# Modulation group 5 is computed in layer 1 in place of block 2

## The chip, the cores and the metric

The kernel runs on one core of a Trainium2 chip. The metric is the device time of one execution in microseconds (us). Five engines work from queues of their own, each strictly in order: TensorE (PE, with PEld for its weight loads), VectorE (DVE), ScalarE (ACT), GpSimd (POOL) and SyncE (SP), which issues nearly all DMA transfers. They wait for each other through semaphores only.

## The reference, cut to what matters

A batch of one sequence with 256 tokens and width 1024 goes through two transformer blocks with a conditioning vector `c` (an NSA attention and a MoBA attention), and then through a third block with windowed and neighbourhood attention and a product-key expert layer (PEER). All is float32. Each norm before a mixer is modulated: a shift and a scale that come from `silu(c) @ w_ada + b_ada` and depend on nothing else.

```python
ada = c_act @ w_ada[layer] + b_ada[layer]
shift1, scale1, gate1, shift2, scale2, gate2 = jnp.split(ada, 6, axis=-1)
h = modulate(rms_norm_2(x, norm1_g[layer]), shift1, scale1)
...
x = x + gate1[:, None, :] * (mixed @ w_out[layer])
h2 = modulate(rms_norm_2(x, norm2_g[layer]), shift2, scale2)
x = x + gate2[:, None, :] * peer(h2, w_query[layer], sub_keys[layer],
                                  u_experts[layer], v_experts[layer])
```

The kernel's modulation group 5 is `shift2, scale2` of this last block: used once, by the norm ahead of `peer`. Group 4 is its gates, used where block 2's output is added to x.

## The kernel before, in words

Four stages follow one another: `layer0` (NSA), `layer1` (MoBA, about 275 to 400 us of the profile), `block2` (to about 540 us) and `peer` (to the end). Tokens are two tiles of 128 rows. Every large product is float32 made of two parts, high and low: a weight tile of 512 KB is loaded (`raw`), ACT casts its high half (`hi`, line 186), DVE subtracts for the low one (`lo`, line 211), and PE runs three matmuls for each product (`mm3`, lines 239 to 241).

Within a stage a list in the table `ORDER` names the steps, and `steps` (line 280) calls them one after the other. A tile scheduler then places the instructions: a step that stands earlier in the list has the earlier priority, and `@n` shifts one by 50 times n. What comes out is one fixed order for each engine. The names in the list that matter here: `z0` to `z3` are the four parts of layer 1's gate projection z, `s...` are attention scores with their softmax, `v..` probabilities times values, `b` the position biases, `o` and `O` the two halves of the output projection. In block 2, `sb0`/`sb1` are the scores and softmax of the neighbourhood attention for the two token tiles (`heads8`, line 1118: scores L1125, row minimum on DVE L1126, exponentials on ACT L1133, normalisation L1139 and L1141), `ob0`/`ob1` their transposes (L1208), copies (L1210) and products with the values (L1214).

`a5` and `a4` are calls of `ada(g)` (line 382), which makes one modulation group: 16 weight tiles of 512 KB, in three buffers (tag `adaw`), each loaded by the SP queue and used by four matmuls into one PSUM tile (`psa`, one buffer); then one DVE addition of the bias, and, for groups 2, 3 and 5, `ada_cols`: four small matmuls (L418), a copy (L422) and a scale (L424).

```python
raw = self.cp.tile([128, 1024], F32, name="adaw", tag="adaw", bufs=CFG["adaw"])
nc.sync.dma_start(raw, a["adaw"][g, k, :, h * 1024:(h + 1) * 1024])            # L391
...
i = nc.tensor.matmul(ps[32 * q:32 * q + 32, ...], self.cond[:, ci + k, :], ...) # L396, 4 for a tile
...
nc.vector.tensor_tensor(r, ps, r, op=OP.add)                                   # L408
```

In the profile one such weight tile is `L396 ... x8` (each of its four float32 matmuls is two records). Both groups 4 and 5 have no input from the token stream, so they can be placed anywhere between the buffers' release and their use.

Of the kernel before, what the change touches and what calls it, by code (L numbers as in the profile page):

```python
# [71 lines left out]
 'cpt0': 2}  # L72
ORDER = {'0': 'pA rt@-4 pB@-4 q0 pC@-2 pG s000 cc z1 ck s001 c00@4 s011 c01 v00 s010 z0 a1@-4 q1 s101@-1 v01@-4 s100 '
      'a2@-4 z2 c10 z3 s110 v10 s111@-2 c11@2 v11 o O a3@-1',
 '1': 'pA@1 q0 s000 s001 v00 q1@-2 s011 s010 v01@-4 z1 s100 z3 s110 s101 z0 z2 b s111 v10@-1 v11@-6 o O',
 '2': 'pA@-2 qa@1 sa0 oa0 kb@-1 qb sa1 oa1 vb tb sb0@5 a4 ob0@1 sb1 a5 o ob1 O@5'}

# [1603 lines left out]
```

## Time and profile before

| | |
|---|---|
| time, median of 3 runs | 1391.27 us (1390.19 to 1397.97) |
| profiled execution, its own time | 1390.83 us |
| its span, first to last instruction | 1389.1 us |
| mean granted PE clock | 0.99 of full speed |
| PE busy | 1339.5 us, 96% of the span |
| DVE busy | 1023.2 us, 74% |
| ACT busy | 820.2 us, 59% |

The share of PE says that the kernel as a whole hangs on PE. It is an average, though: the two places that the change touches have to be read for themselves. In layer 1 at 326 to 354 us PE has hardly a gap. In block 2 it has none before 500 us, some until 517, and a long one at 535 to 540 us, between the last output product and the norm ahead of `peer`.

### The profile page before, as it was taken

The page shows a single profiled execution, that of the slowest core. Times are in us where ns is not written, and L with a number is a line of the kernel's source. Part 1 is how long each engine was busy: PE and PEld are TensorE (multiplying, and loading weights), DVE is VectorE, ACT ScalarE, POOL GpSimd, SP SyncE. Part 2 cuts the span into 40 slices and gives each one's busy share as a digit, 9 for nine tenths or more (in the row PEclk, how much of TensorE's full clock was granted, in tenths as well). Part 3 has the DMA queues.
Part 4 walks back from the last instruction along what each step waited for, and adds up shares of the span by engine and source line. Part 5 has one row for each costly group of instructions (what it writes and reads, how often), then busy time and mean ns, then how long its engine had stood idle before and what let it go on. Part 6 is the DMA issues. An engine that isn't in the chain of part 4 may idle for free.

```text
span 1389.1 us, 25082 instructions
## 1 busy us (share of the span) xinstructions
PE 1339.5 (96%) x8842; PEld 1126.9 (81%) x8842; DVE 1023.2 (74%) x2636; ACT 820.2 (59%) x1887; POOL 21.8 (2%) x27
## 2 busy tenths in 40 slices
PE   6998999999989997999999999999999999999997
PEld 2576775587667756999999999999998888888885
DVE  3595865688576657899999868888866666677777
ACT  3354666367457664555555668888865555555554
POOL 0000000000001100000000000000000000000001
PEclk9999999999999998999999999999999999999999
DMA  8688654742586774555555575455466656667773
GB/s 302 213 283 306 218 188 149 246 157 94 207 296 204 227 236 154 173 179 179 173 180 182 168 217 177 158 166 171 158 224 209 190 192 196 197 222 242 245 242 118
DMA packets 94876, 279.17 MB, mean 201 GB/s; under 512 B 11112, under 2 KB 30320, under 8 KB 94624
## 3 DMA queue, kind: packets, MB, share of 16 engines
q1 hardware_dynamic: 94752, 277.59, 60.6%
q8 instruction: 69, 1.13, 0.3%
q14 instruction: 55, 0.45, 0.1%
HBM read 267.80 MB, written 13.94 MB: 203 GB/s over the span
## 4 chain that ended last, share of the span: by engine, by line
PE 77%; DVE 3%; DMA 2%; ACT 1%; issue 0%; ACTq 0%; DVEq 0%
PE ps L241 18%; PE ps L240 18%; PE ps L239 18%; PE ps L1501 4%; PE acc L241 3%; PE acc L240 3%; PE acc L239 3%; DMA raw<-in_w1o 1%; PE psa L396 1%; PE ps L714 1%; PE ps L525 1%; DVE lo L211 1%; PE ps L709 1%; PE ps L1125 1%; PE ps L639 1%; PE ps L1398 1%
## 5 line engine op out<-in xcount | busy, mean ns | idle before, releaser
L186 ACT CAST hi<-raw 128x512 fp32r<-128x512 f32 (+1 forms) x700 | 429.4, 618 | 350.8 <-PE ps L240 147.8
L211 DVE TENSOR_TENSOR lo<-raw,hi 128x512 fp32r<-128x512 f32 (+1 forms) x700 | 479.8, 688 | 171.2 <-ACT hi L186 158.4
L239 PE MATMUL ps<-hh,hi 128*128 128x256 f32 x1160 | 333.6, 288 | 1.2 <-DVE hh L187 1.2
L240 PE MATMUL ps<-hl,hi 128*128 128x256 f32 x1160 | 329.0, 284 | 1.1 <-DVE hl L211 1.1
L241 PE MATMUL ps<-hh,lo 128*128 128x256 f32 x1160 | 329.0, 284 | 0.0
L239 PEld LDWEIGHTS ps<-hh,hi 128*128 128x128 f32 x1160 | 223.2, 192 | 1.4 <-DVE hh L187 1.4
L240 PEld LDWEIGHTS ps<-hl,hi 128*128 128x128 f32 x1160 | 223.1, 192 | 1.3 <-DVE hl L211 1.3
L241 PEld LDWEIGHTS ps<-hh,lo 128*128 128x128 f32 x1160 | 222.9, 192 | 0.0
L239 PE MATMUL ps<-hi,Ah 128*128 128x512 f32 x508 | 198.1, 390 | 0.0
L240 PE MATMUL ps<-lo,Ah 128*128 128x512 f32 x508 | 197.7, 389 | 0.0
L241 PE MATMUL ps<-hi,Al 128*128 128x512 f32 x508 | 197.6, 389 | 0.0
L240 PEld LDWEIGHTS ps<-lo,Ah 128*128 128x128 f32 x508 | 95.4, 188 | 20.2 <-DVE lo L211 0.2
L239 PEld LDWEIGHTS ps<-hi,Ah 128*128 128x128 f32 x508 | 95.4, 188 | 19.9 <-issue 0.2
L241 PEld LDWEIGHTS ps<-hi,Al 128*128 128x128 f32 x508 | 95.3, 188 | 19.8
L1500 ACT ACTIVATE og<-o,gT 128x128 f32<-128x128 bf16 x256 | 87.2, 394 | 4.1 <-DVE o L1498 0.3
L239 PE MATMUL acc<-hi,hh 128*128 128x512 f32 (+1 forms) x176 | 69.8, 402 | 4.3 <-DVE hh L187 3.1
L240 PE MATMUL acc<-lo,hh 128*128 128x512 f32 (+1 forms) x176 | 70.6, 402 | 2.4 <-DVE lo L211 2.4
L241 PE MATMUL acc<-hi,hl 128*128 128x512 f32 (+1 forms) x176 | 70.2, 400 | 0.0
L1501 PE MATMUL ps<-og,o 128*128 128x128 f32 x512 | 65.1, 275 | 0.0
L1501 PEld LDWEIGHTS ps<-og,o 128*128 128x128 f32 x512 | 61.4, 192 | 0.0
L396 PE MATMUL psa<-adaw,cond 128*32 128x256 f32 x640 | 48.5, 390 | 4.7 <-DMA adaw<-in_adaw 4.3
L1498 DVE TENSOR_TENSOR o<-iof,eT 128x512 bf16<-128x512 f32 x64 | 44.2, 691 | 8.2 <-ACT og L1500 7.5
(397 smaller groups left out, 1937.3 us busy)
## 6 DMA issues: line engine op xcount, KB each, us to landing
raw<-in_u SPq DMA_DIRECT2D x128, 512.0 KB, 3.5
raw<-in_v SPq DMA_DIRECT2D x128, 512.0 KB, 3.5
adaw<-in_adaw SPq DMA_DIRECT2D x86, 512.0 KB, 4.8
raw<-in_w SPq DMA_DIRECT2D x48, 512.0 KB, 3.6
raw<-in_wq SPq DMA_DIRECT2D x16, 512.0 KB, 3.5
zd<-ge SPq DMA_DIRECT2D x56, 128.0 KB, 1.7
ge<-zd SPq DMA_DIRECT2D x56, 128.0 KB, 3.4
raw<-in_adaw SPq DMA_DIRECT2D x10, 512.0 KB, 3.2
```

What stands on the lines that cost most here:

```text
L186: return self.nc.scalar.copy(out, in_)
L211: return self.nc.vector.tensor_tensor(lo, src, hi.bitcast(F32), op=OP.subtract)
L239: mm(out, a[0][asl], b[0][bsl], start=first, stop=False, **kw)
L240: mm(out, a[0][asl], b[1][bsl], start=False, stop=False, **kw)
L241: mm(out, a[1][asl], b[0][bsl], start=False, stop=last, **kw)
L396: i = nc.tensor.matmul(ps[32 * q:32 * q + 32, h * 256:h * 256 + 256], self.cond[:, ci + k, :], raw[:, q * 256:q * 256 + 256], start=(k == ...
L525: self.nc.tensor.matmul(ps[:, k * 128:k * 128 + 128], self.x[t][:, k4 * 512 + k * 128:k4 * 512 + k * 128 + 128], dg, start=(k == 0), stop= ...
L639: nc.tensor.transpose(pr[:P, i * 128:i * 128 + 128], s.rearrange("p a d -> p (a d)") if P == 128 else s, self.identr)
L709: nc.tensor.transpose(ps[:, r * 128:r * 128 + 128], P[a][r][:, br, kb, :], self.c("ident"))
L1498: v.tensor_tensor(o1, iob, eT[0][:, t0:t0 + 4, None].to_broadcast([128, 4, 128]), op=OP.is_equal)
L1500: nc.scalar.activation(og[:, j], o1[:, j], AF.Copy, scale=gT[:, t0 + j:t0 + j + 1])
L1501: nc.tensor.matmul(ps[:, j * 128:j * 128 + 128], o2[:, j], og[:, j], start=(j == 0), stop=(j == 3), skip_group_check=True)
```

## The change

The step `a5` leaves the list of block 2, where it stood behind `sb1`, and enters the list of layer 1, between `z1` and `s100`. The steps themselves are untouched.

```diff
- '1': 'pA@1 q0 s000 s001 v00 q1@-2 s011 s010 v01@-4 z1 s100 z3 s110 s101 z0 z2 b s111 v10@-1 v11@-6 o O',
- '2': 'pA@-2 qa@1 sa0 oa0 kb@-1 qb sa1 oa1 vb tb sb0@5 a4 ob0@1 sb1 a5 o ob1 O@5'}
+ '1': 'pA@1 q0 s000 s001 v00 q1@-2 s011 s010 v01@-4 z1 a5 s100 z3 s110 s101 z0 z2 b s111 v10@-1 v11@-6 o O',
+ '2': 'pA@-2 qa@1 sa0 oa0 kb@-1 qb sa1 oa1 vb tb sb0@5 a4 ob0@1 sb1 o ob1 O@5'}
```

What it does to the order of the engines shows on PE in layer 1. These are the rows before, where scores (`ps<-kT,qT`) and products of z (`acc`) alternate:

```order
1200 L733 MATMUL ps_3558<-kT1_2948,qT_3251 128x256
1201 L240 MATMUL acc_3646<-hl_2868,hi_3699 128x256
1202 L241 MATMUL acc_3646<-hh_2867,lo_3700 128x256
1203 L239 MATMUL acc_3749<-hh_2867,hi_3752 128x256
1204 L240 MATMUL acc_3749<-hl_2868,hi_3752 128x256
1205 L241 MATMUL acc_3749<-hh_2867,lo_3753 128x256
1206 L239 MATMUL acc_3749<-hh_2867,hi_3752 128x256
1207 L733 MATMUL ps_3563<-kT0_2947,qT_3251 128x256
```

And the same place now, with tiles of group 5 (`psa_3717`) between them:

```order
1200 L733 MATMUL ps_3558<-kT1_2948,qT_3251 128x256
1201 L240 MATMUL acc_3646<-hl_2868,hi_3699 128x256
1202 L241 MATMUL acc_3646<-hh_2867,lo_3700 128x256
1203 L396 MATMUL psa_3717<-adaw_3724,cond_82 32x256 x4
1204 L733 MATMUL ps_3563<-kT0_2947,qT_3251 128x256
1205 L733 MATMUL ps_3563<-kT1_2948,qT_3251 128x256
1206 L396 MATMUL psa_3717<-adaw_3730,cond_82 32x256 x4
1207 L733 MATMUL ps_3568<-kT0_2947,qT_3251 128x256
1208 L733 MATMUL ps_3568<-kT1_2948,qT_3251 128x256
1209 L733 MATMUL ps_3585<-kT0_2947,qT_3251 128x256
1210 L733 MATMUL ps_3585<-kT1_2948,qT_3251 128x256
1211 L396 MATMUL psa_3717<-adaw_3736,cond_82 32x256 x4
```

In layer 1, 15 tiles of group 5 (the second to the sixteenth) now stand at rows 1203 to 1318, and L418 follows at row 1324; before there was one tile of group 4 in this place. In turn the 16 tiles of group 4 stand later by two: they take the places that tiles 3 to 16 of group 4 and tiles 1 and 2 of group 5 had. The places of tiles 3 to 16 of group 5, in block 2, are free.

In block 2, before, PE's rows around the first transposes of `ob0` read so (`psa_5525` is group 5, `acc<-hi,ozh0` the first half of the output projection):

```order
1944 L1208 MATMUL ps_5419<-ident_85,P8_5264 128x128 x2
1945 L396 MATMUL psa_5525<-adaw_5586,cond_82 32x256 x4
1946 L1208 MATMUL ps_5419<-ident_85,P8_5264 128x128 x2
1947 L239 MATMUL acc_5706<-hi_5731,ozh0_4461 128x512
1948 L240 MATMUL acc_5706<-lo_5732,ozh0_4461 128x512
1949 L241 MATMUL acc_5706<-hi_5731,ozl0_4462 128x512
1950 L396 MATMUL psa_5525<-adaw_5592,cond_82 32x256 x4
1951 L1214 MATMUL ps_5418<-pt_5424,vb0_4459 64x128 x4
1952 L1208 MATMUL ps_5430<-ident_85,P8_5264 128x128 x4
1953 L1208 MATMUL ps_5441<-ident_85,P8_5264 128x128 x4
1954 L396 MATMUL psa_5525<-adaw_5598,cond_82 32x256 x4
```

Now they read so:

```order
1943 L241 MATMUL acc_5706<-hi_5741,ozl0_4573 128x512
1944 L1125 MATMUL ps_5377<-kT0_4565,qTb0_5339 128x256
1945 L1125 MATMUL ps_5377<-kT1_4566,qTb0_5339 128x256
...
1959 L1125 MATMUL ps_5405<-kT1_4566,qTb0_5339 128x256
1960 L1208 MATMUL ps_5530<-ident_85,P8_5375 128x128 x4
1961 L1214 MATMUL ps_5529<-pt_5535,vb0_4570 64x128 x4
1962 L1208 MATMUL ps_5541<-ident_85,P8_5375 128x128 x4
1963 L1208 MATMUL ps_5552<-ident_85,P8_5375 128x128 x4
1964 L1214 MATMUL ps_5529<-pt_5546,vb0_4570 64x128 x4
```

All 48 products of `o` now come first and without a break (rows 1896 to 1943), then the 16 scores of `sb0`, then `ob0`, then `sb1`, with nothing between them; before, tiles and products were spread among all of these.

On SP, 12 loads of `adaw` now stand between the seventh and the eighth load of z's weights (w1z), and two more behind the eighth, one of them ahead of the output weights w1o. These are the rows:

```order
168 L229 DMA raw_4073<-in_w1z 128x1024 [waits DMAHW5_49,DVE_49]
169 L391 DMA adaw_3742<-in_adaw 128x1024 [waits PE_49]
...
180 L391 DMA adaw_3808<-in_adaw 128x1024 [waits DMAHW2_49,PE_49]
181 L229 DMA raw_4107<-in_w1z 128x1024 [waits DVE_49,Activation_49]
182 L1080 DMA raw_4149<-in_t5c 32x1024 [waits DVE_49]
183 L391 DMA adaw_5427<-in_adaw 128x1024 [waits DMAHW3_49,PE_49]
```

In block 2 the 14 loads of `adaw` that stood between the fourth and the fifth load of the output weights (w2o) are gone from SP.

## Rows read from the trace of the kernel before

**Rows 1.** Page, part 1: busy time, share of the span and instructions by engine.

```profile
PE 1339.5 (96%) x8842; PEld 1126.9 (81%) x8842; DVE 1023.2 (74%) x2636; ACT 820.2 (59%) x1887; POOL 21.8 (2%) x27
```

**Rows 2.** Windows: us; PE, PEld, DVE, ACT, POOL busy; PEclk, DMA share, GB/s.

```profile
326.00:354.40 28.40, 28.32 (x216) 24.62 (x216) 23.39 (x84) 22.93 (x67) 0.00 (x0) 1.00 0.32 114
481.00:512.00 31.00, 30.68 (x261) 18.27 (x259) 12.41 (x44) 14.20 (x36) 0.00 (x0) 1.00 0.86 284
512.00:540.00 28.00, 21.42 (x122) 15.34 (x121) 25.88 (x70) 18.64 (x47) 0.00 (x0) 0.97 0.50 175
```

**Rows 3.** PE timeline, layer 1: start, us, line, operation, tiles, shape, count.

```profile
332.12 0.28 PE L239 MATMUL acc<-hh,hi 128*128 128x256 f32 x1
332.24 0.28 PE L240 MATMUL acc<-hl,hi 128*128 128x256 f32 x1
...
333.24 0.28 PE L239 MATMUL acc<-hh,hi 128*128 128x256 f32 x1
```

**Rows 4.** PE timeline, block 2, 480 to 541 us; in brackets the idle time before.

```profile
480.58 0.47 PE L239 MATMUL acc<-hi,ozh 128*128 128x512 f32 x1
...
482.55 0.40 PE L239 MATMUL acc<-hi,ozh 128*128 128x512 f32 x1
...
483.25 0.39 PE L239 MATMUL acc<-hi,ozh 128*128 128x512 f32 x1
...
488.57 0.39 PE L1125 MATMUL ps<-kT,qTb 128*128 128x256 f32 x1
...
499.05 0.38 PE L1208 MATMUL ps<-ident,P 128*128 128x128 f32 x2
499.36 0.64 PE L396 MATMUL psa<-adaw,cond 128*32 128x256 f32 x8
499.93 0.44 PE L1208 MATMUL ps<-ident,P 128*128 128x128 f32 x2
...
508.21 0.28 PE L1318 MATMUL ps<-cst,osq 128*128 128x1 f32 x2
...
511.28 0.95 PE L418 MATMUL psa<-cst,adar 128*128 128x4 f32 x8
...
517.33 1.24 PE L1208 MATMUL ps<-ident,P 128*128 128x128 f32 x4 [1.22 <-DVE P L1141]
...
540.27 0.98 PE L525 MATMUL ps<-diag,x 128*128 128x128 f32 x3 [4.94 <-DVE rx L274]
```

**Rows 5.** Layer 1's scores on PE, 325.1 to 354.35 us, by line and shape.

```profile
L733 PE MATMUL ps<-kT,qT 128*128 128x256 f32 x24 | 5.0, 295 | 0.0
...
L733 PE MATMUL ps<-kT,qT 128*128 128x128 f32 x16 | 2.8, 285 | 0.1
```

**Rows 6.** The tile `adaw`, 470 to 512 us: from issue to landing.

```profile
DMA to landing us min/median/max: 3.1/4.5/4.7
```

**Rows 7.** ACT timeline, the exponentials of `sb0` and `sb1`.

```profile
489.91 0.51 ACT L1133 ACTIVATE P<-P,nm 128x256 f32<-128x256 f32 x1 [1.43 <-DVE nm L1126]
...
492.35 0.49 ACT L1133 ACTIVATE P<-P,nm 128x256 f32<-128x256 f32 x1
...
492.85 0.49 ACT L1133 ACTIVATE P<-P,nm 128x256 f32<-128x256 f32 x1
...
497.65 0.51 ACT L1133 ACTIVATE P<-P,nm 128x256 f32<-128x256 f32 x1 [1.07 <-DVE nm L1126]
...
511.59 0.51 ACT L1133 ACTIVATE P<-P,nm 128x256 f32<-128x256 f32 x1 [1.54 <-DVE nm L1126]
...
515.40 0.49 ACT L1133 ACTIVATE P<-P,nm 128x256 f32<-128x256 f32 x1
```

**Rows 8.** DVE timeline, block 2: the bias addition of group 5.

```profile
510.38 0.69 DVE L408 TENSOR_TENSOR adar<-psa,adar 128x512 f32<-128x512 f32 x1 [0.78 <-PE psa L396]
```

**Rows 9.** Windows of PE: us, busy, PEclk, DMA share, GB/s.

```profile
398.00:400.00 2.00, 1.75 (x14) 0.65 1.08 362
516.00:518.00 2.00, 0.72 (x4) 1.00 0.00 0
```

## The prediction

> **What bounds the kernel now.** I began with the busy times [rows 1]. PE is busy 1339.5 of 1389.1 us, so at most 50 us of the whole span are not PE's, and a change that only moves PE's work can gain only where PE waits and lose only where it does not. The change removes no instruction. So the second view was the windows over the places where work leaves and where it arrives [rows 2]. Where it arrives, 326 to 354.4 us in layer 1, PE is busy 28.32 of 28.40 us, DVE 23.39 and ACT 22.93. The reader is to see that PE is the full engine there, with the others behind it. Where it leaves, 481 to 512 us in block 2, PE is also full, 30.68 of 31.00, with the transfers at 0.86 of the DMA engines and DVE at only 12.41. The next window, 512 to 540 us, is the opposite: PE 21.42 of 28.00 and DVE 25.88. A full PE has two readings: it may be the bound, or it may be filled with work that could stand anywhere while a chain on other engines sets the pace. The two places differ in this, and the timelines of PE, ACT and DVE tell them apart [rows 3, 4, 7, 8].
>
> **Layer 1: what is added.** The 15 tiles that now stand in this stretch replace one, so 14 are added, and one L418. Between two split products a tile costs this: L240 starts at 332.24 and the L239 that follows the tile and one L241 at 333.24 [rows 3]. That is 1.00 us for two steps that without a tile take 0.12 each (332.12 to 332.24), so the tile takes 0.76. Between scores or transposes it costs 499.93 - 499.36 = 0.57 [rows 4]. By the new order 11 of the 14 stand beside a split product and 3 among scores or transposes: 11 x 0.76 + 3 x 0.57 = 10.1 us. L418 is taken at 0.9 (its own time is 0.95 [rows 4]). Sum 11.0 us.
>
> What could hide part of it is a PE that waits for DVE there without showing it as idle. Only the scores can, since DVE frees their PSUM buffers; they hold PE 5.0 + 2.8 = 7.8 us in all [rows 5]. If a quarter of that is pacing, 2 us are hidden; if nothing, none. I take 0.8, the nearer to the window's full PE.
>
> Two new waits are added. The first is for the weight tiles. Three buffers, and a landing of 3.1 to 4.7 us [rows 6]: at 3.1, near which I put it because the DMA share there is 0.32 and not 0.86 [rows 2], three buffers feed a tile every 1.0 to 1.2 us. The stretch gives 28.4 + 11 us less the part ahead of the first tile, some 20 us for 14 tiles, or 1.4 us each on the mean. It suffices on the mean but not where tiles stand two or three rows apart; I take 0.8 us, with bounds 0 and 4. Queued behind these loads on SP are the eighth w1z load and w1o. The last of the 12 loads must wait for tile 13, some 14 us later than now, and by the order PE first needs the eighth w1z behind the sixteenth tile, so I cost this at nothing; if that cover is missing, one landing of 3 to 5 us is exposed. The second is L408 on DVE, which waits for the sixteenth tile and has scores behind it: in block 2 it waited 0.78 and took 0.69 [rows 8]. PE holds enough products that don't need DVE; 0.2 us, bounds 0 and 1.5.
>
> Layer 1 in sum: 11.0 - 0.8 + 0.8 + 0.2 = +11.2 us, bounds +9 and +15. What follows, the biases, the output projection and the norm of block 2, begins where PE gets through this stretch, so nothing gives it back before block 2. The tiles of group 4 take the places of others of the same kind, tile for tile: nothing.
>
> **Block 2: what is removed.** The same 14 tiles and L418, 11 us of PE. If PE were the bound there to the end, all would come back. But the chain in `sb0`, `ob0`, `sb1` and `ob1` goes over four engines, and the tiles and products stood in its gaps.
>
> First, up to `ob0`. The 48 products of `o` now run in one piece: three take 483.25 - 482.55 = 0.70 us [rows 4], so 11.2. They begin as before at 480.58, plus two tiles that now stand ahead of them (1.1), and end at 493.0 on the clock of before. Only then come the scores of `sb0`, which before began at 488.57. From the first score to the first exponential I take 1.1 (488.57 to 489.91, 1.34, with one product between). Then ACT sets the pace: 0.50 us for each of eight (492.35 to 492.85), so the eighth begins 3.5 us after the first, and from its start to `ob0`'s first transpose pass 499.05 - 497.65 = 1.4 [rows 4, 7]. 493.0 + 1.1 + 3.5 + 1.4 = 499.0, where it stood at 499.05. Gain: 0. Six us of PE's work are gone ahead of this point, and the chain starts as much later.
>
> Second, `ob0`, 499.05 to 508.21, 9.2 us [rows 4]. It is a chain of transposes, copy on ACT, product, four times. Five tiles and five products stand in it. Those that lie under a copy cost nothing; behind a copy's end I count two tiles (0.57 each) and part of a product: gain 1.25.
>
> Third, `sb1`. Before, the first and second exponential were parted by L408 and its tile, and the second began at 511.59, the last at 515.40 [rows 7]. Now: start 1.25 earlier, 506.95; first exponential 1.1 later, seven more at 0.50, and a cast of 0.6 of `ob0`'s result among them: the last begins at 512.3. That is 3.1 earlier, of which 1.85 is new. `ob1` and the rest keep their fillers (the products of `O`) and end as much earlier, with the wait of 4.94 before L525 [rows 4] unchanged, for it is a chain on DVE.
>
> Block 2 in sum: -3.1 us, bounds 0 and -11.
>
> **The sum.** +11.2 - 3.1 = +8.1 us on the profiled execution's own 1390.83 (span 1389.1 and 1.7 around it), which lies 0.44 under the median of 1391.27: 1398.9 us.
>
> **The clock.** At 398 to 400 us the granted clock was 0.65; yet at 516 to 518, where PE was busy 0.72 of 2 us, it kept 1.00 [rows 9]. So gaps of the size that `ob0` and `sb1` get left the clock at the upper of its two levels here, and the sum has no term for it. The Trainium skill speaks against this change at this point ("TensorE: Matmul & The Clock Gate", "HAM oscillation — how this bites in real kernels"): a PE that idles between short bursts finds its clock taken back and runs each next burst at half speed, and it advises to keep matmuls dense. The trace agrees at 400 us and does not at 516. By that rule the result would be the third rival below.
>
> **Rivals.**
>
> First, faster: block 2 gives back nearly all and layer 1 hides part. For it speaks PE at 30.68 of 31.00 up to 512 us [rows 2], with DMA at 0.86, so that the tiles may also have waited for their loads. It needs that `sb0`'s chain starts as early as before. Against it: the new order puts all 48 products ahead of the first score. Price: -11.0 in block 2, +5 to +9 in layer 1: -2 to -6, some 1387. It comes out below 0.5% only if layer 1 hides most of its tiles.
>
> Second, no change: PE is the bound at both ends, +11.2 and -11.0: 1391. For it speaks that PE has no idle record at either place; against it the same order, and that after 512 us it has [rows 2, 4].
>
> Third, slower still: the transposes, products and scores between `ob0` and `ob1`, without fillers, run at half clock. From 499.05 to 517.33 are 18.3 us [rows 4], 15.2 when 3.1 are gone; if a third of that is PE's work at 1.2 GHz instead of 2.4, it takes 5 us more: +13, 1404. It decides from the point at which the gaps let the clock fall. The same time results if the three `adaw` buffers pace layer 1 (the bound of +4 there).
>
> A rival that the change does not do what it says I give no weight: the order shows the tiles moved.
>
> **How the numbers follow.** The forecast has 0.58, the first rival 0.18, the second 0.11, the third 0.13. About 0.5% or 7 us is what a measurement of this kernel tells from no change: 1384.3 and 1398.2. The forecast's own range is 1395 to 1402.5, from its middle bounds (layer 1 +9 to +13, block 2 -2 to -5); 0.6 of it lies above 1398.2. Slower: 0.58 x 0.6 + 0.13 = 0.48. Faster: half of the first rival, 0.09. Same: the rest, 0.43. The range that holds 8 in 10 goes from 1389, which leaves out most of the first rival, to 1404.
>
> **What would show it.** In the profile after, L1084, the first instruction behind the stretch that ends at 354.4 [rows 2], starts 10 to 12 us later, with no idle time of PE for `adaw` over 1 us; L396 there steps by 0.57 to 0.76. The first L1208 of `ob0`, measured from the first product of `o`, stays within 1 us of 499.05 - 480.58 = 18.5; L1318 follows it after 8 us and not 9.2; L525 lies 7 to 9 us later than 540.27. PE shows idle time of some 7 us in block 2 between 493 and 515 that it did not have. I am wrong if L1084 moves by less than 8 us (layer 1 hid work), if `ob0` starts more than 2 us earlier (PE was the bound in block 2), or if the granted clock falls between 495 and 515.

## The result, and the profile after

The changed kernel takes 1409.42 us (median of 11 runs, 1400.26 to 1413.70), the kernel before 1391.04 us beside it (11 runs, 1388.68 to 1397.97). The ratio is 1.0114, 95% interval 1.0096 to 1.0133, so 13 to 19 us slower. The forecast of slower was right, its size was not: 1398.9 was forecast with a range up to 1404.

The page of the changed kernel, part 1, answers to [rows 1]. Its profiled execution took 1410.29 us.

```profile
span 1408.1 us, 25086 instructions
...
PE 1351.8 (96%) x8842; PEld 1137.3 (81%) x8842; DVE 1024.1 (73%) x2636; ACT 822.2 (58%) x1887; POOL 21.9 (2%) x27
```

PE has as many instructions as before, but is busy for 12 us more. The share is again 96%: read alone, it hides both that there is more waiting and that the same matmuls take longer. In layer 1 the first comes from the transfers and the second from the clock. Here is the stretch from the first of the scores (L733) of [rows 5] to L1084 as one window, before and then after (us; PE, PEld, DVE, ACT, POOL busy; PEclk, the granted share of TensorE's full clock; DMA share, GB/s):

```profile
325.10:354.40 29.30, 29.22 (x222) 25.39 (x222) 24.09 (x85) 23.38 (x68) 0.00 (x0) 1.00 0.33 113
```

```profile
327.70:372.70 45.00, 42.06 (x341) 30.74 (x340) 25.32 (x88) 24.94 (x68) 0.00 (x0) 0.92 0.73 237
```

15.7 us longer, where 11.2 were forecast. Idle time of PE is 2.9 us in place of 0.1, the clock is 0.92, and the DMA engines, at a third before, are at 0.73. This is the longest of five executions with the same order in this stretch: the runs e2, e3, e5 and e17 below took 42.1, 44.4, 42.7 and 44.1 us, while without group 5 in it the stretch took 29.3 in each of nine executions. The view of the tile `adaw` in the changed kernel says what PE waits for and how long a load takes (it answers to [rows 6], where the landing was 3.1 to 4.7):

```profile
who waited for it (us, times):
  PEld psa L396: 4.4, 5
  PE psa L396: 2.6, 2
...
DMA to landing us min/median/max: 3.7/5.7/5.9
```

The PE timeline after shows where: the tiles of group 5, two with the wait in brackets, and behind the longer one records of 1.08 us where [rows 4] has 0.64.

```profile
336.25 0.64 PE L396 MATMUL psa<-adaw,cond 128*32 128x256 f32 x8 [0.65 <-DMA adaw<-in_adaw]
...
350.79 1.08 PE L396 MATMUL psa<-adaw,cond 128*32 128x256 f32 x8 [1.99 <-DMA adaw<-in_adaw]
...
354.24 1.08 PE L396 MATMUL psa<-adaw,cond 128*32 128x256 f32 x8
...
372.71 1.02 PE L1084 MATMUL ps<-raw,t5t 32*8 32x512 f32 x2
```

In block 2 the landmarks of [rows 4] now lie so (501.36 is the first product of `o`, 547.49 the end of `ob1`):

```profile
500.36 1.07 PE L396 MATMUL psa<-adaw,cond 128*32 128x256 f32 x16
501.36 0.51 PE L239 MATMUL acc<-hi,ozh 128*128 128x512 f32 x1
...
512.66 0.87 PE L1125 MATMUL ps<-kT,qTb 128*128 128x256 f32 x6
...
518.40 1.43 PE L1208 MATMUL ps<-ident,P 128*128 128x128 f32 x4 [2.71 <-DVE P L1141]
...
527.64 0.38 PE L1318 MATMUL ps<-cst,osq 128*128 128x1 f32 x2 [0.70 <-ACT osq L1313]
...
532.58 2.97 PE L435 MATMUL ps<-adar,cst 128*128 128x512 f32 x4
...
537.00 1.37 PE L1208 MATMUL ps<-ident,P 128*128 128x128 f32 x4 [1.46 <-DVE P L1141]
...
547.49 0.95 PE L1318 MATMUL ps<-cst,osq 128*128 128x1 f32 x8
...
560.89 5.93 PE L525 MATMUL ps<-diag,x 128*128 128x128 f32 x32 [4.94 <-DVE rx L274]
```

From the first L1208 to L525 it takes 42.5 us, where it took 41.2 with six tiles of group 5, L418 and some products of `o` in it; the other eight tiles stood ahead of it. The windows after give the clock (columns as above):

```profile
510.00:520.00 10.00, 6.95 (x33) 4.96 (x31) 5.87 (x23) 7.75 (x24) 0.00 (x0) 0.88 0.41 150
520.00:530.00 10.00, 7.74 (x58) 6.06 (x58) 2.17 (x8) 5.15 (x12) 0.00 (x0) 0.78 0.00 1
530.00:540.00 10.00, 8.07 (x23) 5.14 (x24) 8.93 (x27) 8.51 (x26) 0.00 (x0) 0.73 0.19 54
```

PE is busy for 7 to 8 of 10 us, and part of each window runs at the lower of the two levels.

### The profile page after: what moved, and what is told of

It is laid out like the page before. It is cut to its first block, busy times and chain, and to the rows that moved or that the text cites. A ratio compares the mean times of both kernels' runs of the same rounds, so it can differ in the third digit from the quotient of the medians.

```text
span 1408.1 us, 25086 instructions
## 1 busy us (share of the span) xinstructions
PE 1351.8 (96%) x8842; PEld 1137.3 (81%) x8842; DVE 1024.1 (73%) x2636; ACT 822.2 (58%) x1887; POOL 21.9 (2%) x27
## 4 chain that ended last, share of the span: by engine, by line
PE 76%; DMA 3%; DVE 2%; ACT 1%; issue 0%; ACTq 0%; DVEq 0%
PE ps L240 18%; PE ps L241 18%; PE ps L239 18%; PE ps L1501 4%; PE acc L239 3%; PE acc L241 3%; PE acc L240 3%; DMA adaw<-in_adaw 2%; DMA raw<-in_w1o 1%; PE psa L396 1%; PE ps L525 1%; PE ps L714 1%; PE ps L639 1%; PE ps L709 1%; PE ps L1398 1%; PE ps L1125 0%
## 5 line engine op out<-in xcount | busy, mean ns | idle before, releaser
L211 DVE TENSOR_TENSOR lo<-raw,hi 128x512 fp32r<-128x512 f32 (+1 forms) x700 | 480.1, 689 | 175.4 <-ACT hi L186 159.5
L741 ACT ACTIVATE P<-P,nm 128x128 f32<-128x128 f32 (+1 forms) x96 | 42.7, 446 | 13.2 <-DVE nm L738 12.9
```

Source lines behind the costliest of these rows:

```text
L211: return self.nc.vector.tensor_tensor(lo, src, hi.bitcast(F32), op=OP.subtract)
L741: nc.scalar.activation(Pb, Pb, AF.Exp, scale=-1.0, bias=nm[:, r, br:br + 1], accum_out=sums[:, r, br:br + 1])
```

## The experiments

All times are medians; ratios are to the kernel before on the same chip, with the 95% interval, and differences between two kernels go by these ratios. Lengths of stretches come from one profiled execution of each kernel. Two theories were to be told apart for each end. For block 2: A, its tail hangs on a chain over four engines, the fillers cost nothing there, and without them the clock falls; B, PE bounds it and its 11 us come back. For layer 1: C, three buffers and the transfers pace the tiles, and the clock falls behind the waits; D, it is PE's work alone.

**e1: no group 5 at all.** The list of layer 1 as before, that of block 2 as changed; the norm ahead of `peer` takes group 3's shift and scale in place of group 5's. Against the changed kernel:

```diff
- z1 a5 s100
+ z1 s100
-        gs, sh = self.mods[mod]
+        gs, sh = self.mods[mod] if mod in self.mods else self.mods[3]
```

> Group 5 is left out altogether: the norm ahead of peer uses group 3's shift and scale, and 16 tiles and L418 (11 us of PE) stand nowhere. Layer 1 is then as before and block 2's tail (48 products in one piece, then sb0, ob0, sb1 without fillers) as in the changed kernel. Theory A (the tail hangs on a chain, and without fillers its gaps also let PE's clock fall): the time of before within 4 us, 1387 to 1392, with a granted clock under 0.9 between the first L1208 and L435. Rival B (PE bounds block 2, and the whole loss of the changed kernel comes from layer 1): 11 us less than before, 1380.

Measured: 1391.97 us, ratio 0.9999 (0.9983 to 1.0015). 16 tiles and L418, 11 us of PE's work, are gone, and the time is that of before within 2 us. B has fallen. The windows of e1 show the clock that comes with it:

```profile
500.00:510.00 10.00, 8.14 (x56) 6.60 (x57) 1.37 (x5) 4.48 (x10) 0.00 (x0) 0.67 0.00 1
510.00:520.00 10.00, 8.38 (x24) 5.10 (x24) 9.06 (x26) 8.35 (x27) 0.00 (x0) 0.67 0.16 52
```

So block 2 gives nothing back, the whole difference of the changed kernel is what layer 1 costs, and e2 measures that side.

**e2: group 5 in both layers** (`sb1 a5 o` put back into the list of block 2).

> Group 5 is made twice, in layer 1 and again in block 2 at its old place: layer 1 as in the changed kernel, block 2's tail with its fillers as before. Theory A: the second making costs nothing, since the clock stays at 1.00 in the tail: the time of the changed kernel or up to 4 us less, 1403 to 1409, and what it is above before (13 to 17 us) is layer 1's price alone. Rival B: 11 us more than the changed kernel, 1418 to 1420.

Measured: 1408.31 us, 1.0115 (1.0088 to 1.0142), the changed kernel's time to 0.1%. Making the group a second time costs nothing in block 2 that the interval, some 4 us either way, can show; B's 11 us are out. The 16 us above before are then layer 1's. (In e2's execution 12.8 of them lie in the stretch, and from L1084 to L525 it is 4.2 us longer than before, the changed kernel 2.3; no run tells where these come from.) Its layer 1 has the same order as the changed kernel's, and the comparison of the two executions prices the clock. First e2, then the changed kernel (windows of PE: us, busy, PEclk, DMA share, GB/s):

```profile
345.00:350.00 5.00, 4.00 (x42) 1.00 0.86 283
350.00:355.00 5.00, 4.89 (x49) 1.00 0.97 321
355.00:360.00 5.00, 5.00 (x43) 1.00 0.40 139
```

```profile
345.00:350.00 5.00, 3.67 (x35) 1.00 0.75 227
350.00:355.00 5.00, 4.21 (x26) 0.53 0.83 277
355.00:360.00 5.00, 5.00 (x41) 0.79 0.84 279
```

In e2 PE waited 2.65 us for tiles in three pieces and kept the clock: the stretch took 42.1 us (324.87 to 366.93). The two longer pieces:

```profile
344.98 0.64 PE L396 MATMUL psa<-adaw,cond 128*32 128x256 f32 x8 [0.99 <-DMA adaw<-in_adaw]
...
347.75 0.64 PE L396 MATMUL psa<-adaw,cond 128*32 128x256 f32 x8 [1.00 <-DMA adaw<-in_adaw]
```

In the changed kernel it waited 2.64 in two pieces, the longer 1.99, and lost the clock: 45.0. In the changed kernel's execution some 3 us are the clock's.

**e4: the loads taken away.** Only the first three tiles of group 5 are loaded; the others' matmuls read these again:

```diff
-                raw = self.cp.tile([128, 1024], F32, name="adaw", tag="adaw", bufs=CFG["adaw"])
-                nc.sync.dma_start(raw, a["adaw"][g, k, :, h * 1024:(h + 1) * 1024])
+                raw = keep[(2 * k + h) % 3] if g == 5 and len(keep) == 3 else self.cp.tile(...)
+                if not (g == 5 and len(keep) == 3): nc.sync.dma_start(...); keep.append(raw)
```

> The changed kernel with only the first three tiles of group 5 loaded; the other 13 tiles' matmuls use these three again (group 5's values are therefore not those of the reference). PE's work is the same, the transfers and their waits in layer 1 are gone. Theory C (layer 1 costs more than the 11 us of PE because the three adaw buffers make PE wait, and the clock falls behind that wait): L1084 comes 4 to 6 us earlier than in the changed kernel, no granted clock under 1.00 at 330 to 365 us, time 4 to 6 us less, 1402 to 1405. Rival D (the price is PE's work and the order of scores and products alone): the same time within 2 us.

Measured: 1401.09 us, 1.0065 (1.0042 to 1.0088), 7 us less than the changed kernel by the ratios. The stretch in one window:

```profile
324.40:361.90 37.50, 37.28 (x343) 29.42 (x342) 25.36 (x88) 24.64 (x68) 0.00 (x0) 1.00 0.37 117
```

With the same work PE is full again, at full clock, and the stretch takes 37.5 us: 8.2 for PE's work, and 7.5 of the 15.7 for the transfers and what follows from them, a little more than the 4 to 6 that C expected. Against the four other executions with the loads (42.1 to 44.4) it is 4.6 to 6.9. C holds. (Without loads the order puts eight of the tiles in one piece, which may make them somewhat cheaper.)

**e9 and e10: four buffers** in the changed kernel and, as a control, in the kernel before.

```diff
- 'adaw': 3, ... 'krow2': 2, ... 'pt0': 5
+ 'adaw': 4, ... 'krow2': 1, ... 'pt0': 3
```

> The changed kernel with four adaw buffers in place of three (room made by pt0 5 to 3 and krow2 2 to 1). Theory C (three buffers hold too few transfers under way, a landing of 5.7 us through three buffers gives a tile each 1.9 us): the loads issue every 1.5 us, the wait of PE for adaw goes under 1 us, and from layer 1's first score to L1084 it takes 40 us or less in place of 45. Rival K (the DMA engines are full: a tile of 512 KB takes 1.9 us at some 280 GB/s, however many are under way): landing rises to about 7 us, the loads still issue every 1.8 to 1.9 us, and the stretch takes 42 to 45 us.

> The control of e9: the kernel before with four adaw buffers and the same two cuts. Theory C and rival K alike: within 5 us of before, 1386 to 1396, since in block 2 the tiles' loads are not what bounds; more would mean that the cuts themselves cost.

Measured: e10 1391.25 us, 0.9994 (0.9975 to 1.0012), so the two cuts cost nothing that can be measured here. e9 1405.93 us, 1.0081 (1.0054 to 1.0108), about 4.5 us less than the changed kernel, though the two intervals touch. The issues on SP, first of the changed kernel, then of e9:

```profile
329.55 22.71 SPq L391 DMA_DIRECT2D adaw<-in_adaw  x12
```

```profile
331.59 15.64 SPq L391 DMA_DIRECT2D adaw<-in_adaw  x10
```

From the first issue's start to the last one's this is (22.71 - 0.33) / 11 = 2.03 us for a tile with three buffers and (15.64 - 0.33) / 9 = 1.70 with four; the landing rose from 5.7 to 6.1. The stretch took 40.1 us (329.7 to 369.8), with 14 of the tiles in it and not 15, which is 0.6 to 0.8 us of the gain. This lies between the two theories: a tile each 1.70 us (C 1.5, K 1.8 to 1.9), 40.1 us (C 40 or less, K 42 to 45), a longest wait of 1.43 us for a tile (C under 1). The other executions agree: with three buffers a tile each 1.92 to 2.03 us and a landing of 5.0 to 5.7 (the changed kernel, e2, e3, e5, e17), with four 1.70 and 1.74 and a landing of 6.1 and 5.8 (e9, e11). More buffers help, but with more transfers under way each lands later, so a part of the pace is the transfers' own.

**e3: the products as fillers.** The changed kernel with sb0's scores ahead of o's products:

```diff
- vb tb sb0@5 a4 ob0@1 sb1 o ob1 O@5
+ vb tb sb0 a4 ob0@1 sb1 o ob1 O@5
```

> The changed kernel with sb0 in place of sb0@5 in block 2's list: the scores of sb0 come ahead of o's products, and these 48 products fill the gaps of sb0, ob0 and sb1. Theory A: the tail keeps its clock and its chain starts up to 8 us earlier: 5 to 10 us less than the changed kernel, 1397 to 1403. Rival B: no change beyond 2 us, since the same work stands on PE.

Measured: 1392.18 us, 1.0013 (0.9992 to 1.0034): 14 us less than the changed kernel, more than the 5 to 10 expected; the whole loss is made good. Layer 1's stretch stays as long as it was (44.4 us), so the gain is the tail's alone. PE in e3, to be read against 518.40 and 560.89 above:

```profile
502.39 0.27 PE L1208 MATMUL ps<-ident,P 128*128 128x128 f32 x1
...
511.76 0.28 PE L1318 MATMUL ps<-cst,osq 128*128 128x1 f32 x2
...
542.63 5.83 PE L525 MATMUL ps<-diag,x 128*128 128x128 f32 x32 [4.94 <-DVE rx L274]
```

```profile
500.00:510.00 10.00, 10.00 (x68) 7.54 (x66) 5.11 (x15) 7.80 (x20) 0.00 (x0) 1.00 0.50 154
```

L1084 stood at 368.0, so from there to L525 it is 174.6 us, where before it was 185.9 and after 188.2. The chain begins while 48 products are still to be done, and these lie in its gaps; the clock stays up.

**e6 and e7: the same reordering with group 5 in block 2, and without group 5.**

> The kernel before (group 5 in block 2) with sb0 in place of sb0@5, so that sb0's scores come ahead of o's products. Theory F (e3's 16 us came from starting sb0's chain ahead of the products; with it the tail is bound by PE, and 11 us of tiles cost 11 us there): the tail is as much shorter as in e3 but carries 11 us more, so the time of before within 3 us, 1388 to 1393. Rival G (the tiles still lie in gaps): 8 to 12 us less than before, 1380 to 1384.

> Group 5 left out (peer's norm uses group 3's shift and scale), and sb0 in place of sb0@5. Theory F: 10 to 13 us less than e1 and before, 1379 to 1382, with the clock at 1.00 in the tail; the difference to e6 is then what the tiles cost when PE is the bound, 8 to 11 us. Rival G: within 3 us of e6.

Measured: e6 1390.06 us, 0.9975 (0.9956 to 0.9994); e7 1376.68 us, 0.988 (0.9856 to 0.9904). F holds: once the chain starts early, PE is the bound of the tail, and the tiles that were free in e1 cost 13 us (e6 against e7), a little more than F's 8 to 11; e7 is also lower than F had it. From L1084 to L525 it took 184.9 us in e6, 175.4 in e7, 186.5 in e1, so in these executions the tiles cost 9.5 and the early start is worth 11.1. Of the versions that make all groups, e6 is the only one that came out below both kernels by more than its interval, by a quarter of a percent.

**e8, e11, e12, e14, e15: other places and buffers, all with sb0 early.**

> Group 5 at the end of layer 1's list (behind O), where PE waits twice for more than 2 us at the passage to block 2, and sb0 in place of sb0@5. Theory F: the tiles cost about 11 us there less what lies in the waits, and block 2's tail gives back 11: 1384 to 1391. Theory A alone says nothing here. Rival H (three buffers make PE wait for tiles as in layer 1, and the clock falls): 1392 to 1398.

> The changed kernel with four adaw buffers and sb0 in place of sb0@5. By theory C with F: e3 less 4 to 5 us, 1386 to 1389, which would beat both kernels. By rival K: e3's time, 1390 to 1393.

> Group 5 early in layer 1 (behind q0, its tiles some five PE rows apart from 300 us on) and sb0 in place of sb0@5. There DVE is busier than PE, so part of the tiles may lie in PE's waits. Theory C (loads of 512 KB every 1.9 us at best, and the tiles want one each 1.2 us): the stretch from layer 1's first tile to L1084 is 12 to 16 us longer than before, 1390 to 1394. Rival L (DVE sets the pace there and hides PE's tiles): 4 to 8 us less than before, 1383 to 1387.

> Group 5 in layer 1 behind z2, among the 147 products that need neither DVE nor ACT, four adaw buffers, and sb0 in place of sb0@5. By theory C with F: PE's 9 to 10 us in layer 1 against 11 to 13 in block 2: 1386 to 1390. By rival K (transfers bound the tiles here too, since they stand two to ten rows apart): 1391 to 1396.

> e6 (group 5 in block 2, sb0 in place of sb0@5) with four adaw buffers. By theory C: the waits for tiles in block 2 shrink, 1386 to 1389. By rival K: e6's time, 1389 to 1391.

Measured: e8 1396.27 us, 1.0016 (0.9998 to 1.0034), a miss for F and inside H's range: the waits at the end of layer 1 hid nothing (from L1084 to ob0's first L1208 150.4 us, in e7 135.2; the profiled execution of e8 was its slowest, 1402.24). e11 1391.70, 0.9988 (0.9967 to 1.0008), 3.5 us under e3, less than C's 4 to 5, with intervals that overlap and a time that K's range holds as well; in its trace the stretch of layer 1 is 39.0 us, in e3's 44.4, which speaks for C. e12 1394.21, 1.0016 (0.9998 to 1.0034), at C's upper end. e14 1398.66, 1.0055 (1.0035 to 1.0074), a miss for both: its tiles drew nine loads into the time in which SP should have issued those of layer 1's output weights, and PE stood for these:

```profile
404.47 0.80 PE L239 MATMUL acc<-hi,ozh 128*128 128x512 f32 x1 [10.18 <-ACT hi L186]
```

e15 1394.38, 1.0016 (1.0001 to 1.0031), a miss for both: 5.7 us above e6, with intervals that do not touch, and no run says why the fourth buffer costs here what it did not in e10. So no place in layer 1 was found that beats group 5 in block 2.

**e5, e13: useless matmuls as fillers**, to ask whether the clock or the chain ate the 3.1 us that the forecast gave to block 2 (e5 on the changed kernel, e13 with half as large ones on e1; in both a4 stands ahead of sb0@5, which leaves PE's order as it was):

```diff
-            nc.scalar.activation(P[:, h], P[:, h], AF.Exp, ...)
+            nc.scalar.activation(P[:, h], P[:, h], AF.Exp, ...); sink is None and self.warm(P[:, h])
...
-                        nc.scalar.copy(pt, ps)
+                        nc.scalar.copy(pt, ps); t == 0 and self.warm(P[:, 4 * j2])
```

> The changed kernel's order with small matmuls of no use (128x256 float32, results dropped) put into the gaps of sb0, ob0 and sb1: one behind each exponential and one behind each group of ob0's transposes. The work of the chain is not touched. Theory A (the granted clock, which falls where the fillers are gone, is what ate block 2's gain): clock 1.00 at 500 to 540 us and 2 to 6 us less than the changed kernel, about 1403 to 1407. Rival E (the chain of scores, exponentials and transposes alone, at any clock): clock 1.00 too, but the same time as the changed kernel within 2 us, or more.

> The kernel of e1 (group 5 left out, peer's norm uses group 3) with useless matmuls of 128x128 float32 in the gaps of sb0, ob0 and sb1, behind the exponentials and behind ob0's transposes. Theory A (the fallen clock ate the 3 us): granted clock 1.00 from 490 to 530, and from the first score of sb0 to L525 46 to 47.5 us in place of e1's 49.5; time 2 to 4 us less than e1, 1388 to 1390. Rival E (the chain alone): 49 to 50 us and e1's time within 1.5 us though the clock stays up.

Measured: e5 1405.13 us, 1.0072 (1.0047 to 1.0096); e13 1392.77, 1.0018 (1.0002 to 1.0034). One step is clear in e5, ob0 at a clock of 1.00:

```profile
515.45 0.38 PE L1208 MATMUL ps<-ident,P 128*128 128x128 f32 x2
...
523.63 0.38 PE L1318 MATMUL ps<-cst,osq 128*128 128x1 f32 x2 [0.70 <-ACT osq L1313]
```

8.2 us, against 9.2 after (clock 0.68 over these 9.2 us) and 9.9 in e1 (0.66); 8.0 was forecast. In e13, where more of them stood between the transposes, it took 11.0. As a whole both are inconclusive. The useless matmuls stand in one queue with the scores and delayed these: from the first score to L525 e13 took 51.2 us (496.88 to 548.11, in an execution 7 us above its median), e1 49.5. e5's 6 us under the changed kernel lie partly in a shorter layer 1 (42.7 us in its profile).

**e16, e17: o called ahead of sb1**, without and with group 5 in layer 1. In the changed kernel DVE shows this at the end of sb1:

```profile
534.67 0.69 DVE L187 COPY gate<-ps 128x512 f32<-128x512 f32 x1 [0.71 <-PE ps L435]
...
535.88 0.20 DVE L1136 RECIPROCAL nm<-nm 128x8 f32<-128x8 f32 x1
```

The reciprocal, without which ob1 can't begin, is queued behind the gate copy, and this waits for L435, which at the lower clock takes 2.97 us.

```diff
- ob0@1 sb1 o ob1 O@5
+ ob0@1 o sb1 ob1 O@5
```

> The kernel of e1 (group 5 left out, peer's norm uses group 3) with o called before sb1: L435 and the gate copies come ahead of sb1's scores, and 16 of O's products stand among these. Theory M (in e1 and the changed kernel sb1's reciprocal waits behind the gate copy, which waits for L435): from the first L1318 to ob1's first L1208 8 us or less in place of e1's 9.75, and 2 to 4 us less than e1 in all. Rival E (the exponentials alone): 9 to 9.8 us there, and e1's time within 1.5 us.

> The changed kernel with o called before sb1. Theory M: 2 to 4 us less than the changed kernel, 1404 to 1407, with less than 9 us from the first L1318 to ob1's first L1208 (9.36 in the changed kernel). Rival E: within 2 us of the changed kernel.

Measured: e16 1396.80 us, 1.003 (1.0015 to 1.0045), e17 1411.58, 1.0147 (1.0122 to 1.0171): no gain over e1 and the changed kernel, and 4 to 5 us more than each, with intervals that touch or overlap. M's edit did not take the wait away alone: in e16 it is 14.2 us from the first L1318 to ob1's first L1208, in e1 9.75. The gate copies went ahead, but with them, on DVE, the four additions and updates of x, ahead of sb1's row minima (e16):

```profile
509.35 0.75 DVE L1280 SCALAR_TENSOR_TENSOR acc<-acc,rab,gate 128x512 f32<-128x512 f32 x1
...
513.24 1.28 DVE L1283 TENSOR_TENSOR x<-acc,x 128x512 f32<-128x512 f32 x2
514.44 0.41 DVE L1126 CUSTOM_DVE_ANT_0 P<-ps,bb 128x256 f32<-128x256 f32 x1
```

So neither M nor E is settled by it.

## Why the prediction was wrong, step by step

**What bounds the kernel: right.** A full PE meant two things. In layer 1 it was the bound (e2, e4), in block 2 it was filled (e1). The second reading was the forecast's too; it only did not follow it to its end, zero. That the 11 us are worth nothing belongs to the order that the scheduler made without them, with all products of `o` ahead of sb0's first score: with that score lifted ahead of the products they are worth 13 us (e7 against e6).

**Layer 1, PE's work: forecast +10.4 with L408, measured +8.2** (e4). Of the 11.0 us of tiles and L418 some 2.8 were hidden or cheaper, not 0.8. The loads queued behind the tiles on SP cost nothing in this stretch, as forecast: PE's only two waits there are for `adaw`.

**Layer 1, the wait for tiles: this is the step that failed.** The forecast took 0.8 us with an upper bound of 4, on a landing of 3.1 us, "because the DMA share there is 0.32". That share belonged to a stretch without these loads. With them it was 0.73, the landing 5.7, and three buffers gave a tile each 2.0 us, not each 1.0 to 1.2. [rows 6] had the answer: the same 14 loads, behind the same three buffers, landed at a median of 4.5 in block 2, which through three buffers is 1.5 us a tile, already more than the 1.4 that the forecast had the stretch ask for. The minimum was used where the median stood beside it. Measured, with the clock: 7.5 us (15.7 less 8.2) in this execution and 4.6 to 6.9 in the four others, all above the bound of 4.

**The clock: wrong.** The sum had no term for it, on the window at 516 to 518 us [rows 9] where PE paused and kept it. After a wait of 1.99 us it fell, in layer 1 and again in block 2 after 2.71, which is one of the signs by which the forecast called itself wrong; after waits of up to 1.00 in e2 it did not. But the length of a single wait does not decide it: in e3 the clock was 0.66 at 355 to 360 us, behind five waits of at most 0.88, and the kernel before kept it in layer 1's output projection behind a wait of 2.11:

```profile
385.11 0.50 PE L239 MATMUL acc<-hi,ozh 128*128 128x512 f32 x1 [2.11 <-ACT hi L186]
```

The granted clock was 1.00 from 386 to 388 us there; the same wait in the changed kernel, 2.10 us up to 403.43, was followed by 0.50 at 406 to 408. The Trainium skill says that a PE which waits for transfers between bursts can find its clock taken back, so that the next burst starts at half speed ("TensorE: Matmul & The Clock Gate", "HAM oscillation — how this bites in real kernels"). The trace agrees behind the waits of 1.99 and 2.71 us (a granted 0.50 at 351 to 352 and at 518 to 520 us), not behind the one of 2.11; the forecast had set the rule aside on one window. Why one pause costs the clock and another of the same length does not stays open.

**Block 2, up to ob0: right.** Forecast 0; from the pair of tiles to the first L1208 it took 18.0 us, before 499.05 less 481.21, 17.8. (By its own sign, counted from the first product of `o`, it is 17.0 against 18.5; the sign left out that the pair now stands ahead of that product, which the forecast's sum has.) The two rows of before that this part and the next rest on:

```profile
481.21 1.07 PE L396 MATMUL psa<-adaw,cond 128*32 128x256 f32 x16
...
526.40 0.95 PE L1318 MATMUL ps<-cst,osq 128*128 128x1 f32 x8
```

**ob0 and sb1: forecast -1.25 and -1.85, measured +0.1 and +0.2.** ob0 took 9.2 as before, for the clock took what the fillers gave back (e5: 8.2 at full clock). In sb1 the last exponential did come earlier, counted from L1318 (6.3 us behind it and not 7.2), but the normalisation stood behind the gate copy and L435; that this is the whole cause rests on the trace alone, since e16 changed more than the wait. ob1 came on top: 10.5 us from L1208 to L1318 (537.00 to 547.49), before 9.1 (517.33 to 526.40).

**The sum.** 8.2 + 7.5 + 0 = 15.7; 0.0114 x 1391 = 15.9. Of the 7.6 us that the forecast's 8.1 lacks, 4.5 are layer 1's (6.7 too little for the wait, 2.2 too much for PE's work) and 3.1 block 2's. That 15.7 and 15.9 are so close is in part luck. The spans of the two profiled executions differ by 19.0 us: 2.6 of them ahead of the stretch, where the start lies anywhere from 322 to 330 us in executions of kernels with the same steps up to there, 15.7 in it, 2.3 from there to L525, less 1.6 behind. (The forecast's own range, 1395 to 1402.5, comes to 1394.8 to 1401.8 by the bounds it names, so a half of it and not 0.6 lies above 1398.2.)

**The rivals.** The first (PE gives back nearly all) and the second (zero in sum) fell with e1. The third named both things that went wrong, a falling clock and three buffers that pace layer 1, and it had 0.13 and a price of 13. It took each for the other's alternative, where both came, and it had the clock's cost in block 2 alone: there the clock took back what the fillers gave (ob0), and in layer 1 it added to the waits.

## What to carry to other kernels

A full engine is the bound only if its work, taken out, shortens the stretch: the tiles in block 2 were free in the order that let the chain start late (e1), and they cost 13 us (e7 against e6) once it began early enough. Before such work is moved into a stretch, price its loads by at least the rate that its buffers gave where it stood, not by the quiet of the place to which it goes, and look at what keeps the engine's clock in the place that it leaves. The reordering that paid, e3's one priority, was to start the chain first and let the ready products fill it.

## What the runs showed of the hardware

The same order of PE in layer 1 took 42.1 us in one execution and 45.0 in another, with the same sum of waits: what differed was how the waits lay and whether the clock fell to the lower level. A pause of nearly the same length, at the same instruction, kept the clock in one execution and lost it in another (2.11 us before, 2.10 after; e2 kept 1.00 at 398 to 402 us behind 2.58). The changed kernel's runs spread with the clock: a mean of 0.987 went with the time of 1400.26 us and 0.977 with 1413.70. And with four transfers of 512 KB under way in place of three, each landed later (5.8 and 6.1 us with four, 5.0 to 5.7 with three) while the pace went from 1.92 to 2.03 us for a tile to 1.70 and 1.74.
